# Queries and keys of a hybrid decoder layer projected with features as rows, their head norms taken by a block matrix on TensorE, the stacked layout built by a round trip through DRAM

## The chip, the core and the metric

The kernel runs on one core of a Trainium2 chip. The metric is the time of one execution on the device, in microseconds. A core has TensorE (matrix products; PE in the profile, PEld for its weight loads), VectorE (DVE), ScalarE (ACT), GpSimd (POOL) and SyncE (SP, which issues the DMAs here). TensorE writes PSUM; the others work between PSUM and SBUF. Each engine takes its instructions in a fixed order and waits on semaphores for the others.

## What is computed

One decoder layer over 1024 tokens of width 1024, all in float32. One input projection feeds four mixers, of which differential attention is the one that the change concerns:

```python
h = rms_norm(x, norm1_g)
z = h @ w_in                                  # 1024 x 2304, split into nine parts
q = zq.reshape(b, s, 4, 2, 32)                # 4 heads, 2 maps, 32 features
k = zk.reshape(b, s, 4, 2, 32)
v = zv.reshape(b, s, 4, 64)
...
q = rms_norm(q, q_norm_g)                     # over the 32 features
k = rms_norm(k, k_norm_g)
sc = einsum('bqhmd,bkhmd->bhmqk', q, k) * 32 ** -0.5 + bias      # causal, relative bias
p = softmax(sc)
a = p[:, :, 0] - lam * p[:, :, 1]
o = rms_norm(einsum('bhqk,bkhd->bqhd', a, v), subln_g) * (1 - lam_init)
...
x = x + concatenate([y_pool, y_sconv, y_conf, y_attn]) @ w_out
x = x + (silu(h2 @ w_gate) * (h2 @ w_up)) @ w_down               # h2 = rms_norm(x, norm2_g)
```

## The kernel before

Products keep float32 accuracy by splitting each operand into a rounded part (`hi`) and a remainder (`lo`): `mm3` (L138 to L140) adds hi·hi, hi·lo and lo·hi into one PSUM bank. A weight chunk is loaded by a DMA into `st`, cast to `whi` on ACT (L120), and the remainder `wlo` is made on POOL (L134); there are buffers for three chunks (`wp`, six tiles).

The program goes through these stages: the norm of x and its transposes to `hT`; chunk by chunk (128 features as rows, `wchunk`, `chunk_mm`) the inputs of the conformer, pooling and convolution mixers, with the taps of the depthwise convolution (L317) on DVE as background; then keys, queries and values, each by `proj_tok`, with tokens as rows: for each pair p of token tiles 48 products of 128x256; then attention, 16 units of one pair and one head, into whose gaps products of the output projection (`fillq`, `fill1`, a number from `FQ` at each call) are put; then the second norm and the feed-forward part.

For a pair of keys, `use_k` first calls `ln_pair`, the layer norm of the conformer mixer (transposes into `lnp`, statistics and normalization on DVE, a power on POOL, transposes back, a tanh on ACT), and then `qk_norm`: copy to `qn`, squares, sums over 32 features into a 128x16 tile, the root on POOL (L143, L144), one multiply. Then `stack_T` builds the layout for the scores: for each group g of two heads the four maps are written as 128 columns, the 32 features four times as hi and lo parts (ACT L505, DVE or POOL L506), four 128x128 transposes per token tile on TensorE (L510), and a copy to `KT` (L513). The order of the parts differs between keys (hi, lo, hi, lo) and queries (hi, hi, lo, lo), so that one product over 128 rows gives all four cross terms. Queries go the same way (`use_q`, with the norm weights multiplied in at L530), but only the first pair is stacked before the attention; `prep_q` stacks the others between the units, through PSUM tile `tp` and with calls of `fill1` behind its transposes.

The order on each engine comes from a scheduler of the framework, which ranks by priorities and its own simulated times; DMAs stand in one queue on SP in a fixed order, and each waits there for what it needs.

## Time and profile before

| | us |
|---|---|
| median of 3 runs (lowest, highest) | 1077.91 (1076.92, 1078.37) |
| the profiled execution | 1079.67 |
| its span | 1077.9 |
| TensorE busy | 1047.8 (97%) |
| DVE busy | 736.9 (68%) |
| ACT busy | 439.0 (41%) |
| POOL busy | 223.2 (21%) |

The span is the time from the first to the last instruction of the profiled execution; 1.8 us of it lie around. Busy time of TensorE is that of pipelined products, which overlap: how much one costs is seen from the distance between two starts. A stage is read from its own stretch of the span: which engine has no gap there, and who ends the gaps of the others.

### The profile page before, as it was taken

Reading aid. Unit: us, or ns where it says so; the run is one execution under the profiler, and the core shown is the slowest. Engines: PE = TensorE matmul, PEld = TensorE weight load, DVE = VectorE, ACT = ScalarE, POOL = GpSimd, SP = SyncE. Lnnn points to the kernel's source line nnn. Section 1 sums busy time; section 2 is a strip of 40 time slices with the busy share of each in tenths; the row PEclk is TensorE's granted clock in tenths of the full one; section 3 lists DMA queues with packets and bytes.
Section 4 is the critical chain, followed back from the end, with each engine's and each line's share of the span. In section 5 each row is a group of like instructions: output and inputs, shape, how many; then the busy total and the mean of one; then the engine's idle time right before and its main releaser. Section 6 shows DMA issues by size and latency. Waiting matters only on the chain.

```text
span 1077.9 us, 13508 instructions
## 1 busy us (share of the span) xinstructions
PE 1047.8 (97%) x5203; PEld 876.9 (81%) x5203; DVE 736.9 (68%) x1127; ACT 439.0 (41%) x710; POOL 223.2 (21%) x202
## 2 busy tenths in 40 slices
PE   7999999998989989899999999999999999999998
PEld 6878879996778877788877888888888888888886
DVE  5599995647899966888776776556656567655541
ACT  5512124535786766432332332333333244333320
POOL 5137124655676653000000000000000000000000
PEclk9999999999999999999999999999999999999999
DMA  8131210111021121014576663233223268766731
GB/s 217 49 98 40 59 40 21 40 40 40 30 79 41 50 86 32 6 59 156 220 273 231 218 234 127 59 127 127 88 79 127 102 228 287 261 195 214 230 103 40
DMA packets 89664, 128.04 MB, mean 119 GB/s; under 512 B 17112, under 2 KB 57600, under 8 KB 87040
## 3 DMA queue, kind: packets, MB, share of 16 engines
q1 hardware_dynamic: 89600, 127.18, 35.9%
q8 instruction: 41, 0.67, 0.3%
q14 instruction: 23, 0.19, 0.1%
HBM read 94.13 MB, written 33.04 MB: 118 GB/s over the span
## 4 chain that ended last, share of the span: by engine, by line
PE 74%; DVE 12%; DMA 9%; ACT 2%; issue 1%; POOL 1%; SPq 0%; ACTq 0%; DVEq 0%; POOLq 0%
PE sb L140 8%; PE sb L139 8%; PE sb L138 8%; PE mm L139 6%; PE mm L140 6%; PE mm L138 6%; DMA wd<-in_w_down_dram 4%; PE dx L138 3%; PE dx L140 3%; PE dx L139 3%; DMA dT<-wd 3%; PE dy L138 3%; PE dy L140 3%; PE dy L139 3%; DVE pt L688 1%
## 5 line engine op out<-in xcount | busy, mean ns | idle before, releaser
L138 PE MATMUL sb<-T,rhi 128*128 128x512 f32 x320 | 124.7, 390 | 1.7 <-DVE tp L1030 1.5
L139 PE MATMUL sb<-T,rhi 128*128 128x512 f32 x320 | 124.5, 389 | 0.0
L140 PE MATMUL sb<-T,rlo 128*128 128x512 f32 x320 | 124.3, 389 | 0.0
L911 DVE TENSOR_TENSOR dq<-ds,dq 128x2048 fp32r<-128x2048 f32 x35 | 80.0, 2291 | 61.5 <-ACT dq L910 56.8
L910 ACT CAST dq<-ds 128x2048 fp32r<-128x2048 f32 x35 | 66.9, 1913 | 105.1 <-PE dy L140 38.2
L134 POOL TENSOR_TENSOR wlo<-st,whi 128x1024 fp32r<-128x1024 f32 (+2 forms) x30 | 74.0, 2471 | 109.8 <-ACT whi L120 98.6
L138 PE MATMUL mm<-hT,whi 128*128 128x512 f32 (+1 forms) x224 | 79.6, 367 | 2.3 <-ACT whi L120 1.8
L139 PE MATMUL mm<-hT,whi 128*128 128x512 f32 (+1 forms) x224 | 81.5, 368 | 0.2 <-DVE hT L200 0.2
L140 PE MATMUL mm<-hT,wlo 128*128 128x512 f32 (+1 forms) x224 | 80.7, 364 | 0.4 <-POOL wlo L134 0.4
L138 PEld LDWEIGHTS sb<-T,rhi 128*128 128x128 f32 x320 | 60.1, 188 | 15.0 <-DVE tp L1030 2.5
L317 DVE SCALAR_TENSOR_TENSOR t<-u,cw,t 128x1023 f32<-128x1023 f32 (+28 forms) x58 | 71.4, 1268 | 0.7
L140 PEld LDWEIGHTS sb<-T,rlo 128*128 128x128 f32 x320 | 60.1, 188 | 12.5
L139 PEld LDWEIGHTS sb<-T,rhi 128*128 128x128 f32 x320 | 60.1, 188 | 12.4
L910 ACT CAST rhi<-st 128x1024 fp32r<-128x1024 f32 x28 | 29.5, 1053 | 81.5 <-PE sb L139 49.4
L139 PE MATMUL dx<-dq 128*128 128x512 f32 x160 | 62.2, 389 | 0.0
L140 PE MATMUL dx<-dq 128*128 128x512 f32 x160 | 62.2, 389 | 0.0
L138 PE MATMUL dx<-dq 128*128 128x512 f32 x160 | 61.8, 389 | 0.0
L684 ACT ACTIVATE pt<-sc,mx 128x128 f32<-128x128 f32 (+7 forms) x64 | 47.7, 748 | 18.5 <-DVE mx L681 18.4
L138 PE MATMUL mm<-whi,hT 128*128 128x256 f32 x192 | 54.9, 289 | 0.0
L139 PE MATMUL mm<-wlo,hT 128*128 128x256 f32 x192 | 54.6, 285 | 0.0
L140 PE MATMUL mm<-whi,hT 128*128 128x256 f32 x192 | 54.4, 284 | 0.0
L138 PEld LDWEIGHTS mm<-hT,whi 128*128 128x128 f32 x224 | 42.0, 192 | 10.0 <-ACT whi L120 2.1
(342 smaller groups left out, 2679.6 us busy)
## 6 DMA issues: line engine op xcount, KB each, us to landing
ds<-dL SPq DMA_DIRECT2D x35, 512.0 KB, 4.2
wd<-in_w_down_dram SPq DMA_DIRECT2D x10, 1024.0 KB, 5.0
dT<-wd SPq DMA_DIRECT2D x10, 1024.0 KB, 4.0
dL<-afs SPq DMA_DIRECT2D x10, 1024.0 KB, 4.4
ds<-dT SPq DMA_DIRECT2D x20, 512.0 KB, 6.0
st<-in_w_in_dram SPq DMA_DIRECT2D x18, 512.0 KB, 3.8
st<-in_w_gate_dram SPq DMA_DIRECT2D x15, 512.0 KB, 3.8
st<-in_w_up_dram SPq DMA_DIRECT2D x15, 512.0 KB, 3.7
```

The lines of the kernel that those rows point to most:

```text
L134: G.tensor_tensor(lo[:, nv:], st[:, nv:], hi[:, nv:].bitcast(F), op=ALU.subtract)
L138: T.matmul(ps, lhsT=L[0], rhs=Rr[0], start=first, stop=False, skip_group_check=more)
L139: T.matmul(ps, lhsT=L[0], rhs=Rr[1], start=False, stop=False, skip_group_check=more)
L140: return T.matmul(ps, lhsT=L[1], rhs=Rr[0], start=False, stop=last, skip_group_check=more)
L317: V.scalar_tensor_tensor((z if s == 30 else acc)[:, s:], u[:, :S - s], w[:, 30 - s:31 - s], acc[:, s:], op0=ALU.mult, op1=ALU.add)
L684: A.activation(pts[m][:, 0:w], sc[:, 0:w], AF.Exp, bias=mx, scale=-1.0, accum_out=lt[:, h, m, i:i + 1])
L688: V.scalar_tensor_tensor(pts[0][:, 0:w], pts[1][:, 0:w], cf, pts[0][:, 0:w], op0=ALU.mult, op1=ALU.add)
L910: A.copy(hi, src)
L911: (eng or V).tensor_tensor(lo, src, hi.bitcast(F), op=ALU.subtract)
```

## The change

Keys and queries are projected by `wchunk` and `chunk_mm`, like the other mixers, with 128 features (one group of two heads) as rows and 512 tokens as columns. There are eight such tiles: keys, then queries, each for two groups and two halves of the tokens. The mean square over 32 features is a product with `onr`, a 128x128 matrix of four blocks of 1/32, twice for the hi and lo part of the squares. From it come a root on ACT, a reciprocal on DVE and one further correction step of it (the factor -3 is taken up by the constant 0.25 in `gq`, with the sign). The tile is split into hi and lo, written to DRAM (`kq`), and read back in the stacked order, by four DMAs of 256 KB into `KT` or by eight of 128 KB into `QT`; all eight tiles of `QT` are there before the attention. `qk_norm`, `stack_T`, `prep_q` and the tiles `qn` of the projections go; in the attention the calls of `fill1` that stood in `prep_q` stay. The split tiles use, in turn, the memory of `VV3` and that of `mh` and `ml`; the small `qn` of the attention output takes over a used tile of `QT`. `padl` holds EPS and serves as bias.

```diff
-    gq, gk = bc("gq", q_g, 32, const), bc("gk", k_g, 32, ctp)
-    V.scalar_tensor_tensor(gq, gq, -(32 ** -0.5), gk, op0=ALU.mult, op1=ALU.mult)
+    gq, gk = const.tile([P, 32], F, name="gq")[:, 0:1], ctp.tile([P, 1], F, name="gk")
+    for i in range(4):
+        dma(out=gq[32 * i:32 * (i + 1), :], in_=q_g.rearrange("o p -> p o"))
+        dma(out=gk[32 * i:32 * (i + 1), :], in_=k_g.rearrange("o p -> p o"))
+    V.scalar_tensor_tensor(gq, gq, -0.25 * 32 ** -0.5, gk, op0=ALU.mult, op1=ALU.mult)
...
-    qtp = mid.enter_context(pool("qtp", 2))
+    qtp = mid.enter_context(pool("qtp", 8))
     kvp = mid.enter_context(pool("kvp"))
-    VV = [kvp.tile([P, 2, 4, 128], R, name=f"VV{p}") for p in range(4)]
-    qn = [kvp.tile([P, 2, 256], F, name=f"qn{p}") for p in range(4)]
+    VV = [kvp.tile([P, 2, 4, 128], R, name=f"VV{p}", tag=f"VV{p}") for p in range(3)]
+    QT = {(p, g): qtp.tile([P, 4, 256], R, name="QT", tag="QT") for p in PO for g in range(2)}
...
+    for m in range(4):
+        G.memset(onf[32 * m:32 * (m + 1), 32 * m:32 * (m + 1)], 1.0 / 32)
+    A.copy(onr, onf)
...
+    def heads(c0, isq, order, each=None):
         for g in range(2):
+            W = wchunk(c0 + g * P)
+            for h in order:
+                ps = ps_mm()
+                chunk_mm(W, ps, h, 0, 0, 512)
+                if each:
+                    each(2 * g + h)
+                sh = sm.tile([P, 512], R, name="sh", tag="kn")
+                sl = sm.tile([P, 512], R, name="sl", tag="sq")
+                sq = spp.tile([P, 512], F, name="sqt", tag="sp")
+                A.activation(sh, ps, AF.Square)
+                A.activation(sq, ps, AF.Square)
+                V.tensor_tensor(sl, sq, sh.bitcast(F), op=ALU.subtract)
+                ss = ps_t2()[:, 0:512]
+                T.matmul(ss, lhsT=onr, rhs=sh, start=True, stop=False)
+                T.matmul(ss, lhsT=onr, rhs=sl, start=False, stop=True)
+                r = spp.tile([P, 512], F, name="rt", tag="sp")
+                A.activation(r, ss, AF.Sqrt, bias=padl[:, 0:1])
+                V.reciprocal(r, r)
+                r2 = sq
+                A.activation(r2, r, AF.Square)
+                if isq:
+                    V.scalar_tensor_tensor(r, ps, gq, r, op0=ALU.mult, op1=ALU.mult)
+                else:
+                    V.tensor_tensor(r, ps, r, op=ALU.mult)
+                V.scalar_tensor_tensor(r2, ss, padl[:, 0:1], r2, op0=ALU.add, op1=ALU.mult)
+                V.scalar_tensor_tensor(r, r2, -3.0, r, op0=ALU.add, op1=ALU.mult)
+                n = nh[0]
+                nh[0] += 1
+                hl = (kvp if n % 2 else misc).tile([P, 2, 512], R, name="khl", tag="VV3" if n % 2 else "mh")
+                A.copy(hl[:, 0], r)
+                V.tensor_tensor(hl[:, 1], r, hl[:, 0].bitcast(F), op=ALU.subtract)
+                dma(out=kq[n].rearrange("s p t -> p s t"), in_=hl.bitcast(F))
+                for b in range(2):
+                    for a in range(2):
+                        o = slice(64 * a + 32 * b, 64 * a + 32 * b + 32)
+                        src = kq[n, a if isq else b].rearrange("(m d) t -> d m t", m=4)
+                        if isq:
+                            for k in range(2):
+                                dma(out=QT[2 * h + k, g][o].bitcast(F), in_=src[:, :, 256 * k:256 * (k + 1)])
+                        else:
+                            dma(out=KT[g][o, :, 512 * h:512 * (h + 1)].bitcast(F), in_=src)
...
-    proj_tok(C_K, use_k)
-    proj_tok(C_Q, use_q, PO)
-    for g in range(2):
-        prep_q(PO[0], g, ps_t2, 4)
+    heads(C_K, False, range(2), ln_pair)
+    heads(C_Q, True, range(2))
+    VV.append(kvp.tile([P, 2, 4, 128], R, name="VV3", tag="VV3"))
     proj_tok(C_V, use_v)
...
         if h == PQ1 and j > 0:
-            prep_q(p, 1, ps_tp, 4, fill1)
+            for k in range(2):
+                fill1(marks[-1])
         if h == PQ0 and j < 3:
-            prep_q(PO[j + 1], 0, ps_tp, 4, fill1)
+            for k in range(2):
+                fill1(marks[-1])
         unit(u, p, h)
```

How the instructions stand now is seen at three places. On ACT, before, in the middle of the keys (line numbers of the kernel before; `kst` is the stacked tile, `t` its transpose, `sq` the squares):

```order
L562 ACTIVATE th<-lnp,lb,lg 128x256
L505 CAST kst<-qn_1380 128x8x32 x3
L562 ACTIVATE th<-lnp,lb,lg 128x256
L120 CAST whi<-st 128x1024 x2
L488 COPY qn_1382<-mm 128x512
L505 CAST kst<-qn_1380 128x8x32
L513 CAST KT_1364<-t_1606 128x4x128
L513 CAST KT_1364<-t_1615 128x4x128
L490 ACTIVATE sq<-qn_1382 128x512
```

ACT in the changed kernel (its own line numbers), from the squares of the second key tile to those of the third (`rt` is the root, `khl` the split tile):

```order
L510 ACTIVATE sh<-mm 128x512
L511 ACTIVATE sqt<-mm 128x512
L573 ACTIVATE th<-lnp,lb,lg 128x256
L517 ACT_TABLE_LOAD
L517 ACTIVATE rt<-t_1545,padl 128x512
L520 ACTIVATE sqt<-rt 128x512
L530 CAST khl<-rt 128x512
L573 ACT_TABLE_LOAD
L573 ACTIVATE th<-lnp,lb,lg 128x256
L510 ACTIVATE sh<-mm 128x512
```

Before, work of two pairs was interleaved on ACT; now the squares of a tile stand behind the copy of the tile before, with two table loads in between.

DVE in the changed kernel, from the first reciprocal to the second (`b`, `mv`: statistics of the layer norm):

```order
L518 RECIPROCAL rt<-rt 128x512
L559 BN_AGGR mv<-b_1516 128x2
L559 BN_AGGR mv<-b_1519 128x2
L524 TENSOR_TENSOR rt<-mm,rt 128x512
L525 SCALAR_TENSOR_TENSOR sqt<-t_1467,padl,sqt 128x512
L564 TENSOR_SCALAR ln<-lnp,mv,rs 128x256 x2
L526 SCALAR_TENSOR_TENSOR rt<-sqt,rt 128x512
L531 TENSOR_TENSOR khl<-rt,khl 128x512
L574 TENSOR_SCALAR mixC<-lnp,lg,lb 128x256
L575 SCALAR_TENSOR_TENSOR mixC<-th,mixC 128x256
L512 TENSOR_TENSOR sl<-sqt,sh 128x512
```

The multiply at L524 is the last reader of the projection's bank `mm`; the difference `sl` of the next tile stands behind all that belongs to this one.

TensorE before, around one pair of keys:

```order
L138 MATMUL mm<-whi,hT_101 128x256
L510 MATMUL t_1606<-ident,kst 128x128 x4
L510 MATMUL t_1615<-ident,kst 128x128 x4
L139 MATMUL mm<-wlo,hT_101 128x256
L140 MATMUL mm<-whi,hT_102 128x256
```

TensorE in the changed kernel, at the second key tile's sums (`t_1545`); 22 products of a later tile stand between the last rows shown and the next transposes L568:

```order
L140 MATMUL mm<-hT_103,wlo 128x512
L568 MATMUL lnp<-ident,ln 128x128 x4
L514 MATMUL t_1545<-sh,onr 128x512
L515 MATMUL t_1545<-sl,onr 128x512
L555 MATMUL lnp<-ident,mixC 128x128 x4
L138 MATMUL mm<-hT_101,whi 128x512
```

The transposes of the stacked tiles are gone; the products with the block matrix stand in their place, each behind an operation of ACT or DVE of the same tile.

## Rows read from the trace of the kernel before

**Rows 1.** Page, part 1: busy us, share of the span, instructions

```profile
PE 1047.8 (97%) x5203; PEld 876.9 (81%) x5203; DVE 736.9 (68%) x1127; ACT 439.0 (41%) x710; POOL 223.2 (21%) x202
```

**Rows 2.** Windows: projection stretch, attention; busy us and count by engine, clock, DMA

```profile
163.00:244.00 81.00, 81.00 (x686) 80.76 (x685) 42.73 (x85) 37.17 (x75) 45.94 (x37) 1.00 0.10 33
244.00:410.00 166.00, 154.26 (x852) 126.52 (x851) 144.39 (x366) 115.40 (x266) 102.43 (x100) 0.99 0.17 55
```

**Rows 3.** Timeline of PE in the key projection: start us, duration us, instruction

```profile
180.17 0.28 PE L140 MATMUL mm<-whi,hT 128*128 128x256 f32 x1
180.29 1.03 PE L510 MATMUL t<-ident,kst 128*128 128x128 f32 x8
181.08 0.36 PE L138 MATMUL mm<-whi,hT 128*128 128x256 f32 x1
```

**Rows 4.** Timeline of PE in the chunk projections, 512 columns

```profile
101.22 0.39 PE L138 MATMUL mm<-hT,whi 128*128 128x512 f32 x1
101.45 0.39 PE L139 MATMUL mm<-hT,whi 128*128 128x512 f32 x1
```

**Rows 5.** Groups of PE by form: count, busy us, mean ns, idle before, releaser

```profile
L138 PE MATMUL mm<-whi,hT 128*128 128x256 f32 x192 | 54.9, 289 | 0.0
L510 PE MATMUL t<-ident,kst 128*128 128x128 f32 x80 | 10.8, 272 | 0.0
L510 PE MATMUL tp<-ident,kst 128*128 128x128 f32 x48 | 7.4, 276 | 2.6 <-POOL kst L506 2.6
```

**Rows 6.** Groups of DVE by form

```profile
L536 DVE TENSOR_TENSOR VV<-mm,VV 128x512 fp32r<-128x512 f32 x4 | 2.8, 690 | 9.4 <-ACT VV L535 9.4
L759 DVE SCALAR_TENSOR_TENSOR ml<-tp,subg,mh 128x512 fp32r<-128x512 f32 x4 | 3.0, 746 | 1.1 <-ACT mh L758 1.1
L547 DVE BATCH_NORM_STATS2 b<-lnp 128x6 f32<-128x256 f32 x8 | 3.0, 420 | 1.4 <-PE lnp L544 1.4
L686 DVE RECIPROCAL cf<-lt 128x1 f32<-128x1 f32 x32 | 4.9, 154 | 0.4 <-ACT pt L684 0.3
L349 DVE TENSOR_TENSOR nlam<-es 128x1 f32<-128x1 f32 x1 | 0.1, 148 | 0.0
L350 DVE TENSOR_SCALAR nlam<-nlam 128x1 f32<-128x1 f32 x1 | 0.1, 144 | 0.0
```

**Rows 7.** Groups of ACT by form, then its timeline at the table load

```profile
L490 ACT ACTIVATE sq<-qn 128x512 f32<-128x512 f32 x8 | 5.1, 635 | 0.1
L562 ACT ACTIVATE th<-lnp,lb,lg 128x256 f32<-128x256 f32 x8 | 4.5, 569 | 6.1 <-PE lnp L557 6.0
...
423.62 1.05 ACT L120 CAST whi<-st 128x1024 fp32r<-128x1024 f32 x1 [1.19 <-DMA st<-in_w_up_dram]
424.69 1.28 ACT L917 ACT_TABLE_LOAD   x1
425.99 0.60 ACT L917 ACTIVATE tp<-pg 128x512 f32<-128x512 f32 x1
```

**Rows 8.** Windows behind pauses of TensorE; the column before the last two is the clock

```profile
248.00:252.00 4.00, 2.46 (x11) 1.30 (x10) 3.45 (x12) 1.46 (x7) 2.32 (x3) 1.00 0.19 66
252.00:256.00 4.00, 4.00 (x16) 3.54 (x16) 2.41 (x12) 2.56 (x9) 1.22 (x1) 0.57 0.02 6
```

**Rows 9.** DMA issues (count, KB, us to landing), and SP issuing four

```profile
dL<-afs SPq DMA_DIRECT2D x10, 768.0 KB, 3.3
tr<-scr SPq DMA_DIRECT2D x4, 128.0 KB, 3.3
...
72.66 1.77 SPq L381 DMA_DIRECT2D tr<-scr  x4
```

**Rows 10.** Waits in the attention: us in total, times, longest

```profile
PE tp L510 <- POOL kst L506: 2.6, 3, 1.1
```

**Rows 11.** Chain of waits, 244 to 404 us: first and last piece of the query layout

```profile
264.44 0.70 POOL kst L506
...
354.80 0.44 PE tp L510 x4
```

More of the change, by code (lines that the diff above doesn't have):

```diff
@@ L89, in tile_hybrid @@
     sm = ctx.enter_context(pool("sm"))
-    padl = sm.tile([P, 16], F, name="padl")
+    padl = sm.tile([P, 48], F, name="padl")
     padr = ctx.enter_context(pool("padr", side="right")).tile([P, 56], F, name="padr")
@@ L738, in unit @@
             G.tensor_tensor(rrf, rrf, mhalf[:, 0:8], op=ALU.pow)
+            qn[p] = qtp.tile([P, 2, 256], F, name=f"qn{p}", tag="QT")
             (G if X5[PO.index(p)] else V).tensor_tensor(qn[p].rearrange("p i (h d) -> p (i h) d", h=4), of, rrf.unsqueeze(2).broadcast_to([P, 8, 64]),
@@ L754, in out_attn @@
         yield tr
-        mh = misc.tile([P, 2, 256], R, name="mh", tag="mh")
-        ml = misc.tile([P, 2, 256], R, name="ml", tag="ml")
+        mhl = misc.tile([P, 2, 2, 256], R, name="mh", tag="mh")
+        mh, ml = mhl[:, 0], mhl[:, 1]
         psv = ps.rearrange("p (a b) -> p a b", a=2)
```

46 lines of the change are left out of this document (7 added, 39 removed).

## The prediction

> **What bounds the kernel now.** I read the busy times first, then busy time by stretch, then the order of the instructions, and last the chain of waits of the one stretch that the change also touches. TensorE is busy in 97% of the span [rows 1]; a change pays where it takes columns from TensorE, or a wait from in front of it. The stretch in which queries, keys and values are projected runs from 163.4 us, the first key product, to 244 us, the first score product. In it TensorE never stops (81.00 of 81.00 us) while DVE works 42.73 and ACT 37.17 us [rows 2]. So this stretch costs what TensorE is given there, 80.6 us, and the other two engines have about 40 us of slack each. The attention behind it (244 to 410) is mixed: TensorE 154.26 and DVE 144.39 of 166 us [rows 2]. The feed-forward part, 668 us, is not touched.
>
> **What leaves TensorE.** A product over 256 columns starts 0.12 us after the one before, one over 512 columns 0.227 us (0.23 between two rows; 24 products take 5.45) [rows 3, 4]. Queries and keys now take 384 narrow products, 46.1 us, and will take 192 wide ones, 43.6: 2.5 us less. The transposes of the stacked layout take 0.79 us for eight, 0.87 with the slower first product behind them, so 0.11 each [rows 3]; 80 of them stand in the projection stretch and 48 in the attention [rows 5]: 8.8 and 5.3 us less. Sixteen products with the block matrix come in, 3.6 us more. The demand on TensorE in the projection stretch thus falls by 7.7 us, to 73. If TensorE stayed the bound, that would be the result there.
>
> **What comes to DVE and ACT.** It does not stay the bound. Before, the norm of a group works on sums of 32 (a 128x16 tile), with the root on POOL. Now every one of the eight 128x512 tiles passes a chain at full width: two squares on ACT, their difference on DVE, two products, a root on ACT, a reciprocal on DVE, a square on ACT, three more DVE operations, a copy on ACT, a difference on DVE. The order shows ACT strictly in turn: the squares of the next tile stand behind the copy of this one, and a table is loaded before the root and again before the tanh of the layer norm, eight loads more than before.
>
> The price on which all rests is the reciprocal over 512 elements; no row shows one. The one-element RECIPROCAL takes 154 ns, other one-element operations 144 to 148 [rows 6]. If those 6 to 10 ns are paid once, 512 elements cost what another operation of that size costs, 0.69 us [rows 6]; if they are paid for each element, 3.1 to 5.1 us come on top: 3.8 to 5.8. The others, of two kinds, differ among themselves by 4 ns, and the reciprocal stands apart from both; a surcharge that belongs to the operation is more likely to come with each element than once, so I take an excess of 7 ns, near their mean, per element: 4.3 us. Both ends stay for the range. The Trainium skill, VectorE: DVE Perf Modes, section "First, the fixed hardware budget", says that this operation divides iteratively with a repeat count of 8; by its clock of 0.96 GHz (Trainium Kernel Development and Optimization, section "NeuronCore Architecture") that makes an estimate of 512 x 8 / 0.96 = 4.3 us, the same.
>
> **The projection stretch after the change**, step by step, counted from 163.4:
> - The first root stands on ACT behind the cast of the third weight chunk from there, which waits until the second tile's products release a weight buffer: 48 x 0.227 = 10.9, cast 1.05, table 1.28 [rows 7], root 0.6 (as the square, 635 ns [rows 7]), reciprocal 4.3: 18.1 us.
> - Then three key tiles, each a loop. The reciprocal frees the PSUM bank through one multiply (bank statistics of the layer norm 0.9 and the multiply 0.7 [rows 6]); only then do the 22 products of a later tile run that stand in TensorE's order ahead of the layer norm's transposes (5.0, and 0.6 for the transposes); then tanh, square, square, tanh on ACT (0.5 each), table 1.28, root 0.6, reciprocal 4.3: 15.5 us. Three make 46.5, and 1.0 for one more cast in the first. TensorE needs 6.8 us for a tile: it pauses some 6 us in each loop.
> - Then three query tiles, bound by DVE: 0.69 + 4.3 + 0.75 (with a pointer and from PSUM [rows 6]) x 2 + 0.69 x 2, less 0.3 of overlap = 7.6 each: 22.8. Then the last tile's difference and its ones product, 1.6.
> - Behind that product stand 144 of the 192 value products: 17.3 and 1.3 of waits for banks: 18.6.
> Sum: 18.1 + 47.5 + 22.8 + 1.6 + 18.6 = 108.6 us in place of 80.6: **28 us more**. Each microsecond of the reciprocal is worth seven in this sum. With 0.69 us the first part is 14.5, the loops 11.9 each (36.7 with the cast), the query tiles are bound by TensorE (24 x 0.227 + 0.45 = 5.9 each, 17.7), and the sum is 89.1: 8.5 more. With 5.8 it is 119: 38 more.
>
> The pauses have a second price. From 248 to 252 TensorE was busy for 2.46 of 4 us, and from 252 to 256 its granted clock was 0.57 of full, near the lower of its two levels of 1.2 and 2.4 GHz [rows 8]: 1.7 us lost. Three loops with a pause of 6 us each may lose this three times: **5 us** (0 to 7).
>
> **The round trip.** A tile is written by one DMA of 512 KB and read by four (keys) or eight (queries). DMAs of 768 and 128 KB land after 3.3 us, and SP needs 1.77 us to issue four [rows 9]. So a key tile takes SP about 9 us and a query tile about 11, within the 15.5 of a loop, while query tiles come every 7.6 and queue up: the last is written some 9 us after it is ready. SP waits here for each write before its reads, and behind it queue loads of w_out and the x rows of the partial output projection (not wanted until 10 us into the attention). The scores of the first two heads need the first query tile, some 30 us old by then; those of the other two need the third, which lands about when the stretch ends and is wanted 10 us later. The last buffer of the values shares its memory with odd tiles and waits for the last write, which ends within 1 or 2 us of the last value product. I take **1 us** for this and the exponential's table load together (0 to 4).
>
> **The attention.** Out go 48 transposes, the POOL differences and the ACT copies around them, and with them waits of TensorE for POOL of 2.6 us [rows 10]. In the chain of waits of this stretch thirteen pieces belong to the query layout, 6.0 us together; the first and the last stand in [rows 11]. DVE loses only two operations of 0.4 and stands next in that chain nearly everywhere, so part comes back as waits for DVE: **4 us less** (0 to 10).
>
> The first load of the norm weights, eight tiny DMAs for two, is at 25 us on a queue that waits later anyway: nothing; uncovered it would be 3 us. Both fill slots of a removed layout step are still called: nothing, within 1 us.
>
> **Rivals.**
> - *The reciprocal runs at the ordinary rate.* Stretch +8.5, clock 2, attention -4, start 1: +7.5 us, 1085. For it: nothing shows the long form. Against: the one-element row.
> - *TensorE runs ahead and stays the bound* (faster). Three PSUM banks let it work three tiles ahead, which hides a chain of up to 16 us; then only its demand counts: -7.7, and -6 in the attention: 1064. It decides if the chain of a tile takes less than the 6.8 us of TensorE's work. Against: the in-order ACT queue ties tiles together, and even at 0.69 us the loop is 11.9.
> - *A table switch costs more than the load.* The row shows 1.28 us, with 0.02 us between the cast before it and the load [rows 7]. If the pipe had to empty unseen, each loop, the first root and the exponential would be longer by as much as the load again: five times 1.3, near +7: 1115. The Trainium skill, ScalarE: Activation LUTs, section "What ACT_TABLE_LOAD costs", counts 1.38 us of drain on top of the load for every switch, and its section "Table sets: the hidden batching unit" advises against alternating sets as this change does; the trace's gap does not bear the drain out.
> - *The round trip ends last.* If reads into 32 partitions land in twice the time, the attention waits for its third and fourth heads' queries: some +12 on the forecast, 1120.
>
> **How the numbers follow.** The profiled execution took 1079.7 us (span 1077.9), 1.8 above the median of the runs, 1077.9. Sum: 28 + 5 + 1 - 4 = +30; 1079.7 + 30 = 1109.7, less the 1.8: **1108 us**. Chances: forecast 0.68 (1092 to 1124, reciprocal from 3 to 5.8), ordinary reciprocal 0.14, TensorE as the bound 0.09, table switch 0.05, round trip 0.04. The range goes from the ordinary reciprocal less a bit of attention, 1084, to 1124. About 0.2% can be told from no change here; of the third case 0.02 and of the second 0.01 lie within it, so faster 0.07, same 0.03, slower 0.90.
>
> **What would show it.** A RECIPROCAL row of about 4.3 us, eight of them; DVE busy over 75 us in the projection stretch, and TensorE idle there for some 25 us with waits for ACT and DVE; ACT_TABLE_LOAD rows of 1.28 us, ten in all; a stretch of about 110 us; the attention a few us shorter. Wrong would make it: a reciprocal below 1 us, a PE row that never waits between 165 and 245, or an attention that gains over 10 us.

## The result, and the profile after

The changed kernel takes 1118.73 us (median of five runs, 1116.0 to 1119.61) against 1077.91 (1076.39 to 1078.86) for the kernel before on the same chip: 1.0378 times as long, with an interval of 1.0361 to 1.0396. The forecast was 1108.0 with a range of 1084 to 1124. The profiled execution took 1117.67 us, its span 1115.9.

Three stretches divide the part that matters: the projections (first key product to first score product), the attention (to the first product of the feed-forward part) and the rest (to the end of the span). The first is counted from 163.4 us in every run; the first key product starts at 162.85 us in the kernel before, at 163.10 in the changed one, and between 161.98 and 164.34 in the runs below. Stretches are those of one profiled execution, which for three of the runs (the layer norm moved, the transposes back, the old order) took some 3 us more than the median of the run. A difference of 1 or 2 us between two stretches therefore says nothing.

| stretch, us | before | after | change | forecast |
|---|---|---|---|---|
| projections | 80.6 | 111.8 | +31.2 | +28, clock +5, start +1 |
| attention | 171.6 | 179.6 | +8.0 | -4 |
| rest | 662.3 | 661.1 | -1.2 | 0 |
| span | 1077.9 | 1115.9 | +38.0 | +30 |

The page's first part answers to [rows 1]. TensorE has 304 instructions less and is busy 5 us longer:

```profile
PE 1052.9 (94%) x4899; PEld 864.5 (77%) x4899; DVE 766.0 (69%) x1135; ACT 437.1 (39%) x679; POOL 188.0 (17%) x179
```

The windows of the two stretches after the change (busy us and count of PE, PEld, DVE, ACT and POOL, then the granted clock) answer to [rows 2]:

```profile
163.40:275.20 111.80, 85.96 (x430) 70.36 (x429) 73.55 (x94) 42.82 (x65) 17.34 (x19) 0.86 0.43 126
275.20:454.80 179.60, 159.77 (x829) 126.63 (x828) 147.91 (x374) 111.95 (x253) 95.62 (x92) 0.98 0.18 56
```

In the projections TensorE now stands idle for 25.8 us, where it never stopped before, and runs at a mean clock of 0.86 of full. DVE's work went from 43 to 74 us. The new operations, by form (busy us, mean ns, idle time before them and its releaser), on DVE and ACT:

```profile
L518 DVE RECIPROCAL rt<-rt 128x512 f32<-128x512 f32 x8 | 26.8, 3345 | 2.3 <-ACT rt L517 2.3
...
L517 ACT ACT_TABLE_LOAD x4 | 5.1, 1283 | 0.1
```

The reciprocal takes 3.35 us, five times an ordinary operation of its size. TensorE's waits from 160 to 285 us (us in total, times, longest) name the chain of the norm in all three of their first lines:

```profile
PE mm L138 <- DVE rt L524: 11.6, 3, 5.3
PE t L515 <- DVE sl L512: 8.6, 5, 5.1
PE t L514 <- ACT sh L510: 4.9, 4, 2.9
```

The first of the three loops of the keys, in the chain of waits (start us, us, what). It begins and ends with the multiply that frees the PSUM bank:

```profile
182.13 0.70 DVE rt L524
...
188.47 1.04 ACT whi L120
189.53 1.28 ACT L573
190.82 0.56 ACT th L573
191.39 0.49 ACT sh L510
191.88 0.49 ACT sqt L511
192.36 0.46 ACT th L573
192.83 1.28 ACT L517
194.13 0.70 ACT rt L517
194.85 3.35 DVE rt L518
198.20 0.61 DVE b L558 x2
198.95 0.66 DVE rt L524
199.66 0.79 PE mm L138
200.45 0.43 PE mm L139
```

From multiply to multiply 16.8 us pass: a cast of weights, a table load, a tanh of the layer norm, the squares of the next tile, a tanh, the second load, root, reciprocal. The other two loops take 16.0 and 17.9 us, and in them only the load before the root is in the chain. TensorE's timeline has three pauses in the first, 8.5 us together (start us, us, instruction, idle time before it and its releaser):

```profile
191.93 0.50 PE L514 MATMUL t<-sh,onr 128*128 128x512 f32 x1 [2.87 <-ACT sh L510]
193.14 0.79 PE L515 MATMUL t<-sl,onr 128*128 128x512 f32 x1 [0.71 <-DVE sl L512]
...
199.66 0.79 PE L138 MATMUL mm<-hT,whi 128*128 128x512 f32 x1 [4.87 <-DVE rt L524]
```

The last two rows of the chain show a second price: products of 512 columns follow one another at 0.43 us instead of 0.23 [rows 4], five of them here. The windows there show why (clock in the column before the last two):

```profile
191.00:195.00 4.00, 2.15 (x6) 1.20 (x6) 2.66 (x6) 3.79 (x6) 0.93 (x1) 0.69 1.05 254
195.00:199.00 4.00, 0.00 (x0) 0.00 (x0) 4.00 (x6) 0.63 (x1) 0.00 (x0) 0.50 0.25 91
199.00:203.00 4.00, 3.34 (x8) 2.67 (x9) 3.32 (x7) 1.18 (x2) 0.88 (x2) 0.53 0.00 0
```

With TensorE half busy and then not at all, its clock is granted at the lower of its two levels, and stays there for some microseconds of the work that follows (0.50 and 0.53 in the last two windows). Busy time times the missing share of the clock, summed over windows of 4 us of the whole stretch, makes 8.4 us. I call that sum the clock loss below. Stretch less idle time less clock loss is what TensorE's work takes at full clock: 111.8 - 25.8 - 8.4 = 77.6.

In the attention TensorE's waits are these (275 to 455 us):

```profile
PE sc L684 <- ACT pt L695: 8.3, 11, 1.9
PE tp L710 <- DVE pt L699: 4.6, 5, 2.5
```

The waits for POOL of [rows 10] are gone, and more has come in their place. Before, the same two waits took 1.5 and 1.8 us (244 to 416 us):

```profile
PE tp L699 <- DVE pt L688: 1.8, 4, 0.8
PE sc L673 <- ACT pt L684: 1.5, 2, 0.8
```

TensorE's idle time in the attention rose from 12.3 to 19.8 us and its clock loss from 1.7 to 2.8; the first of these has to be explained, since the change takes 48 transposes and two DVE operations out of there and puts nothing in.

### The profile page after: what moved, and what is told of

The parts are those of the page before. It is cut to its first block, busy times and chain, and to the rows that moved or that the text cites. A ratio compares the mean times of both kernels' runs of the same rounds, so it can differ in the third digit from the quotient of the medians.

```text
span 1115.9 us, 12964 instructions
## 1 busy us (share of the span) xinstructions
PE 1052.9 (94%) x4899; PEld 864.5 (77%) x4899; DVE 766.0 (69%) x1135; ACT 437.1 (39%) x679; POOL 188.0 (17%) x179
## 4 chain that ended last, share of the span: by engine, by line
PE 73%; DVE 12%; DMA 7%; ACT 4%; issue 3%; POOL 1%; SPq 0%; ACTq 0%; DVEq 0%; POOLq 0%
PE sb L138 9%; PE sb L139 9%; PE sb L140 9%; PE mm L138 5%; PE mm L140 5%; PE mm L139 5%; PE dx L138 3%; PE dx L140 3%; PE dx L139 3%; DMA wd<-in_w_down_dram 3%; PE dy L140 2%; PE dy L138 2%; DMA dT<-wd 2%; PE dy L139 2%; DVE rt L518 2%
## 5 line engine op out<-in xcount | busy, mean ns | idle before, releaser
L138 PE MATMUL mm<-hT,whi 128*128 128x512 f32 (+1 forms) x288 | 108.5, 386 | 13.4 <-DVE rt L524 11.6
L139 PE MATMUL mm<-hT,whi 128*128 128x512 f32 (+1 forms) x288 | 108.7, 380 | 0.4 <-DVE hT L200 0.2
L140 PE MATMUL mm<-hT,wlo 128*128 128x512 f32 (+1 forms) x288 | 108.0, 377 | 0.3 <-POOL wlo L134 0.3
L138 PEld LDWEIGHTS mm<-hT,whi 128*128 128x128 f32 x288 | 55.8, 198 | 25.2 <-DVE rt L524 13.2
L140 PEld LDWEIGHTS sb<-T,rlo 128*128 128x128 f32 x320 | 60.5, 189 | 12.6
L139 PEld LDWEIGHTS mm<-hT,whi 128*128 128x128 f32 x288 | 56.7, 197 | 10.6 <-DVE hT L200 1.4
L140 PEld LDWEIGHTS mm<-hT,wlo 128*128 128x128 f32 x288 | 56.6, 196 | 9.9 <-POOL wlo L134 0.6
L120 ACT CAST whi<-st 128x1024 fp32r<-128x1024 f32 x28 | 29.4, 1049 | 60.0 <-PE mm L139 44.6
```

Of the source, the lines that this page charges most:

```text
L120: A.copy(dst, src)
L138: T.matmul(ps, lhsT=L[0], rhs=Rr[0], start=first, stop=False, skip_group_check=more)
L139: T.matmul(ps, lhsT=L[0], rhs=Rr[1], start=False, stop=False, skip_group_check=more)
L140: return T.matmul(ps, lhsT=L[1], rhs=Rr[0], start=False, stop=last, skip_group_check=more)
```

## Experiments

All times are compared with runs of the kernel before on the same chip (medians 1076.5 to 1078.0). The edits are to the changed kernel unless another is named.

**The reciprocal.** It is left out; everything else stays.

```diff
                 A.activation(r, ss, AF.Sqrt, bias=padl[:, 0:1])
-                V.reciprocal(r, r)
```

> The changed kernel with the reciprocal left out (the root itself goes on; this part of the computation is missing). The projection stretch (first key product to first score product) was 80.6 us before and is 111.8 with the change; the reciprocal takes 3.35 us there. Theory A, the stretch is a chain tied together by DVE and ACT in order: seven reciprocals lie on it, so 7 x 3.35 = 23.4 us go as long as the chain stays the bound, plus 2 to 4 us of granted clock that comes back with shorter pauses: a stretch of 84 to 90 us, total 1091 to 1098. Rival B, the pauses belong to the round trip through DRAM and to the lower clock, and the reciprocal hides beside them: under 8 us less, total over 1110.

Measured: 1107.87 us, ratio 1.0286 (1.0266 to 1.0305); stretches 98.8, 181.7, 662.2. The windows of the projections and of the place shown above:

```profile
163.40:262.20 98.80, 84.87 (x430) 70.20 (x429) 47.38 (x87) 42.78 (x65) 17.97 (x19) 0.88 0.48 143
...
191.00:195.00 4.00, 1.92 (x7) 1.40 (x5) 3.89 (x8) 1.55 (x4) 0.83 (x1) 0.60 0.55 165
195.00:199.00 4.00, 4.00 (x11) 3.08 (x11) 1.60 (x3) 1.84 (x2) 0.88 (x2) 0.54 0.34 131
```

The stretch stays far above the one expected. Without the reciprocal 13.0 us of stretch go, 3.9 for each of its microseconds and not seven. TensorE's idle time falls by 11.9, to 13.9, but the clock loss does not fall at all (8.9): the pauses that remain are enough to bring the clock down. 18 us of the 31 remain without any reciprocal. The run changes the order too: by the two timelines about one in nine of TensorE's instructions of the stretch and one in five of DVE's stand in another place, so the 13.0 us are not the price of the reciprocal alone.

**The table loads.** The root becomes a square, so that no set has to be changed between root and tanh.

```diff
-                A.activation(r, ss, AF.Sqrt, bias=padl[:, 0:1])
+                A.activation(r, ss, AF.Square, bias=padl[:, 0:1])
```

> The changed kernel with the root replaced by a square (the right root is missing from the computation), which needs no other function table: eight table loads go, the reciprocal stays. Theory A: the loads of 1.28 us that lie on the chain go, by the trace six of them (one before the first root, one before the first tanh, three before roots, one before the first exponential): 6 to 9 us less, total 1109 to 1113. Rival, a switch drains the pipe and costs twice its row: 13 us or more, total under 1106. Rival, the loads hide beside DVE: under 2 us.

Measured: 1115.23 us, ratio 1.0351 (1.0329 to 1.0373); stretches 110.4, 178.8, 660.7. Seven loads of 1.28 us stood in the stretch and all of them go. The median falls by 3.5 us, which lies between the expectations, the stretch by 1.4 (0.6 when each is counted from its own first key product, 162.32 and 163.10). The order on TensorE, ACT and DVE is nearly the same. The loads stand in the chain above, yet hardly count: when they go, TensorE's wait for DVE's `sl` rises from 8.6 to 10.2 us. Another link was nearly as late; the chain of the second loop now passes through DVE, where `sl` stands behind the end of the layer norm:

```profile
207.72 0.42 DVE mixC L575
208.15 0.67 DVE sl L512
```

In the same loop eleven products follow one another at 0.43 us, where there were five with the loads: part of what the loads gave back went to the clock.

**The layer norm, moved.** Its four pairs go into the values, one with each pair of value tokens.

```diff
     def use_v(p, ps):
...
+        ln_pair(p)
...
-    heads(C_K, False, range(2), ln_pair)
+    heads(C_K, False, range(2))
```

> The changed kernel with the four layer norms called with the value tiles instead of the key tiles; the result is the same. Theory A: the loop of a key tile (16 to 18 us) is tied by ACT, where the layer norm's tanh stands between the squares and the root, and by its table loads; without it key tiles run like query tiles, at 6.3 to 8.3 us, so three loops give back 25 us, the layer norms find 40 us of DVE time under the value products: a stretch of 82 to 90 us, total 1090 to 1098. Rival B, the round trip and SP's queue set the pace (a key tile every 16 us): no gain, total over 1112.

Measured: 1108.69 us, ratio 1.0283 (1.0262 to 1.0304); stretches 91.0, 192.2, 663.3. The stretch of the projections came out just above the 82 to 90 us expected, with 11.6 idle and a clock loss of 5.8. But the scheduler put the last two layer norms into the attention, and there 12.6 us were lost, with the clock at its lower level from 264 to 284 us (windows of that time):

```profile
264.00:274.00 10.00, 7.75 (x29) 6.20 (x30) 8.88 (x40) 5.69 (x21) 1.23 (x4) 0.50 0.00 1
274.00:284.00 10.00, 8.21 (x28) 6.42 (x27) 9.40 (x36) 5.35 (x18) 4.06 (x7) 0.50 0.01 2
```

So the layer norm beside the keys is behind half of the 34 us of idle time and clock loss: 17 are left without it. That it acts through the order on ACT and TensorE is what the chain above shows for one loop; this run also takes half of the layer norms' work out of the stretch, and doesn't tell the two apart.

**The layer norm, first.** All four pairs ahead of the keys.

```diff
-    heads(C_K, False, range(2), ln_pair)
+    for p in range(4):
+        ln_pair(p)
+    heads(C_K, False, range(2))
```

> The changed kernel with all four layer norms called ahead of the key tiles, and none beside them; the result is the same, two of the table loads and the loop through tanh are gone. With the layer norms among the value tiles the stretch fell to 91.0 us, but half of them spilled into the attention, at the lower clock, and that took the gain back. Here nothing can spill. Theory A: the layer norms, one after the other, hold the first root back by some 12 us, then eight tiles follow at DVE's 6.9 us each (reciprocal 3.35, five operations of 0.7), then the value products: a stretch of 92 to 98 us, the attention as with the change (178 to 182), total 1098 to 1105. Rival: the spilled layer norms were not the reason and the attention grows again by over 8 us: total over 1107.

Measured: 1116.87 us, ratio 1.0378 (1.0345 to 1.041); stretches 110.6, 178.9, 660.5. The eight tiles then took about what was expected, 7.3 us each for 6.9 (58.2 from the first reciprocal at 202.99 to 261.2). But the layer norms in a row wait for one another, and TensorE has nothing else to do:

```profile
183.00:203.00 20.00, 6.22 (x19) 3.42 (x19) 10.34 (x26) 6.60 (x12) 1.76 (x4) 0.60 0.01 1
```

The gain and this gap cancel but for 1.2 us of stretch, and the 92 to 98 us expected were missed. The attention did not grow, as the expectation had it.

**Keeping TensorE busy.** Sixteen products without use behind the sums of the first three key tiles, to tell idle time from clock.

```diff
-                ss = ps_t2()[:, 0:512]
+                t2 = ps_t2()
+                ss = t2[:, 0:512]
...
+                if not isq and 2 * g + h < 3:
+                    for k in range(16):
+                        T.matmul(t2[:, 512:1024], lhsT=onr, rhs=sl, start=True, stop=True)
```

> The changed kernel with 16 products more behind the sums of each of the first three key tiles, into a half of a PSUM tile that nobody reads: 48 x 0.227 = 10.9 us of work added to TensorE, in the pauses of some 5 us behind which its clock was 0.50 to 0.53 of full. Theory A: the pauses' second price is the clock; kept busy, TensorE runs the 22 products behind each pause at full clock: each loop 1.5 to 2 us shorter, total 1112 to 1115 in spite of the added work. Rival: the clock is low there for another reason, or the loop does not hang on it: no change or up to 5 us longer.

Measured: 1132.69 us, ratio 1.0519 (1.0494 to 1.0545); stretches 123.8, 182.5, 659.3. Rows of TensorE's timeline (the added products) and of ACT's (the root) show that it tested something else:

```profile
195.90 5.44 PE L519 MATMUL t<-sl,onr 128*128 128x512 f32 x16
```

```profile
201.38 0.69 ACT L521 ACTIVATE rt<-t,padl 128x512 f32<-128x512 f32 x1 [4.84 <-PE t L519]
```

The root reads the first half of the PSUM tile, and waited 4.84 us for products into its second half. The chain was lengthened, and the wait behind it remained. The run tells nothing of the clock.

**The output products that fill gaps.** Twelve calls of the attention get two products more, taken from three late calls. `FQ` is the table of counts; of the six pairs of raised entries the diff shows one, and the three late ones.

```diff
-FQ = [..., 4, 0, 0, 0, 0, 6, ..., 14, 6, 0, 1, 12, 2, 1, 9, ..., 20]
+FQ = [..., 4, 0, 2, 2, 0, 6, ..., 8, 6, 0, 1, 6, 2, 1, 9, ..., 8]
```

> The changed kernel with 24 products of the output projection moved, in the table of numbers, to the six places in the attention where the query transposes stood (two at each of the twelve calls), taken from three late places; the result is the same. The attention (first score product to first feed-forward product) took 171.6 us before and takes 179.6 with the change, though 5.3 us of transposes left it. Theory C: the transposes had stood in gaps where TensorE would have waited, and the table of fill products was fitted to the old gaps; with products put there the attention falls by 3 to 7 us, total 1111 to 1115. Rival D: the attention is longer because something comes late from the projections (query tiles, weight chunks, the x rows behind them on SP's queue): within 1 us of no change, or longer.

Measured: 1130.25 us, ratio 1.0487 (1.0468 to 1.0506); stretches 113.1, 175.4, 677.3. The attention got 4.2 us shorter up to the first feed-forward product, and the rest 16 longer: the products taken from the late calls are missing there (TensorE's clock is 0.61 and 0.54 from 460 to 480 us, 1.00 behind the same point of the changed kernel), and the last product with the values ended at 462.6 us instead of 441.2. Places for fill are not interchangeable.

**Transposes back in the attention.** The removed transposes, with their copies and differences, are put back at their six places on other data.

```diff
+    def old_prep(x3):
+        for i in range(2):
+            st = spp.tile([P, 4, 128], R, name="kst", tag="sp")
...
+            ps = ps_tp()
+            for a in range(4):
+                ins = T.transpose(ps[:, a * P:(a + 1) * P], st[:, a, :].bitcast(F), ident)
+            fill1(ins)
+            A.copy(st, ps.rearrange("p (a b) -> p a b", a=4))
...
-            for k in range(2):
-                fill1(marks[-1])
+            old_prep(X3[2 * j + 1])
```

> The changed kernel with idle work put back into the attention where the query layout stood: at the six places the ACT copies, the DVE or POOL differences and 48 transposes of the kernel before, on data that nobody needs (one buffer is shared with other work, which before it was not). Theory C: what was taken out had cost next to nothing, so putting it back costs next to nothing or helps: attention 170 to 180 us (179.6 without), total 1108 to 1118. Rival D: the attention is long for another reason, and the work put back comes on top: 183 us or more, total over 1121.

Measured: 1117.25 us, ratio 1.0375 (1.0357 to 1.0394); stretches 112.6, 180.1, 662.6. 48 transposes more cost 0.5 us of attention, less than can be told. TensorE is busy 4.2 us longer and idle 3.6 us less (16.2): they fill waits. The attention doesn't go back to 171.6 either, so their number is not what lengthened it.

**The kernel before, with its queries laid out early.** The old operations, transposes included, but all before the attention.

```diff
-    qtp = mid.enter_context(pool("qtp", 2))
+    qtp = mid.enter_context(pool("qtp", 8))
...
         qv = qk_norm(ps, new_qn(p).rearrange("p a b -> p (a b)"))
...
+        for g in range(2):
+            prep_q(p, g, ps_t2, 4)
...
-            prep_q(p, 1, ps_tp, 4, fill1)
+            for k in range(2):
+                fill1(marks[-1])
```

> The kernel before with one part of the change alone: all eight stacked query tiles are built ahead of the attention, by its own path (tokens as rows, transposes on TensorE, no DRAM), in the buffers of the changed kernel (eight query tiles, norm tiles in shared memory); the attention is the changed kernel's. Theory C: the attention is longer because the transposes had stood in gaps of TensorE and the table of fill products was fitted to them: 178 to 183 us here too, in place of 171.6; the projections 5 to 8 us more (48 transposes of 0.11 moved there); total 1088 to 1096. Rival D: the changed kernel's attention suffers from what the projections hand over late: here it takes 165 to 172 us, total 1077 to 1085.

Measured: 1100.7 us, ratio 1.023 (1.0209 to 1.025); stretches 91.9, 181.8, 661.4. Neither round trip nor block matrix is in this kernel, and its attention loses as much as the changed one's:

```profile
255.30:437.10 181.80, 161.96 (x829) 128.82 (x828) 148.41 (x374) 110.92 (x253) 96.76 (x93) 0.96 0.16 50
```

What lengthens the attention is something that both share: the layout work is gone from it, and with it the order may have changed. The next run separates the two.

**The old order in the attention.** The changed kernel, in which each engine takes its instructions of the attention in the order of the kernel before (without those that no longer exist).

```diff
+ORD = {
+    "PE": [0, 1, 2, 3, 4, 5, 6, 7, 15, 14, 8, ...],
...
+    for eng, want in ORD.items():
+        q = [i for i in traced[first:] if str(i.engine) == "EngineType." + eng]
+        for u, v in zip(want, want[1:]):
+            tc.add_manual_dep(q[v], q[u].name, mybir.DependencyInfo(mybir.DependencyClass.NoSync, mybir.DependencyReason.DATA), reason="order")
```

> The changed kernel with the attention's instructions put, engine by engine, into the order of the kernel before (less those of the query layout), by edges that fix nothing but the order of issue; nothing else is changed, the result is the same. The attention took 171.6 us before, 179.6 with the change, 181.8 in the kernel before with its query tiles built early, 180.1 with the transposes put back: neither the projections nor the missing work explain the 8 us. Theory F: the scheduler put the attention into another order once the layout steps were gone, and the tables of fill products fit the old one: with the old order 165 to 172 us, total 1103 to 1111. Rival G: the waits come with the missing steps whatever the order: 177 us or more, total over 1115.

Measured: 1103.49 us, ratio 1.0248 (1.0227 to 1.027); stretches 108.1, 170.0, 663.5. The same instructions take 9.6 us less in the attention:

```profile
271.50:441.50 170.00, 155.65 (x830) 125.36 (x828) 146.84 (x374) 112.19 (x253) 95.98 (x92) 0.99 0.21 63
```

By the timelines, some 590 of 800 instructions of TensorE in the attention stand in the changed kernel in the sequence of the kernel before, and nearly all in this run. Its timeline shows it at one place, the same in both (start us, us, instruction, idle time before it). The changed kernel:

```profile
330.19 0.46 PE L684 MATMUL sc<-KT,QT 128*128 128x512 f32 x1
330.48 0.34 PE L719 MATMUL av<-at,VV 128*128 128x256 f32 x2
330.68 0.41 PE L710 MATMUL tp<-ident,pt 128*128 128x128 f32 x2
332.95 0.62 PE L684 MATMUL sc<-KT,QT 128*128 128x512 f32 x2 [1.87 <-ACT pt L695]
```

With the old order:

```profile
325.05 0.60 PE L690 MATMUL sc<-KT,QT 128*128 128x512 f32 x2
325.48 0.34 PE L725 MATMUL av<-at,VV 128*128 128x256 f32 x2
325.67 0.28 PE L716 MATMUL tp<-ident,pt 128*128 128x128 f32 x1
325.70 0.59 PE L690 MATMUL sc<-KT,QT 128*128 128x512 f32 x2
```

In the first, two transposes (`tp`) stand in a row, and the score products behind them wait 1.87 us for ACT's exponential to leave their buffer; in the second, transposes and pairs of score products alternate, and nothing waits at this place. Over the whole attention the wait for ACT falls from 8.3 to 6.4 us and that of `tp` for DVE from 4.6 to 1.1; idle time (14.4) and clock loss (1.6) together make 6.6 of the 9.6 us. The projections became 3.7 us shorter as well, though nothing ahead of the attention was set and the order on TensorE and ACT is the same. 1.0 of it is the beginning (the first key product starts at 162.11), and 1.8 is one operation of DVE (`rt<-sqt,rt`, L526 of the changed kernel, at 248.69), which takes 0.69 us here and took 2.48 there, beside POOL's remainder of a weight chunk (248.22, 2.40 us).

**A narrow norm.** The sums are taken with tokens as rows (a 128x16 tile), the root on POOL in place of ACT and DVE, spread by ACT and turned by four transposes. This and the next two runs keep the old order in the attention.

```diff
-                T.matmul(ss, lhsT=onr, rhs=sh, start=True, stop=False)
-                T.matmul(ss, lhsT=onr, rhs=sl, start=False, stop=True)
+                for b in range(4):
+                    for k, q in enumerate((sh, sl)):
+                        T.matmul(t2[:, 4 * b:4 * b + 4], lhsT=q[:, b * P:(b + 1) * P], rhs=onr[:, 0:P:32], start=k == 0, stop=k == 1)
...
+                G.tensor_tensor(rr, rr, mhalf[:, 0:16], op=ALU.pow)
+                A.copy(sq.rearrange("p (m d) -> p m d", d=32), rr.unsqueeze(2).broadcast_to([P, 16, 32]))
+                for b in range(4):
+                    T.transpose(t2[:, 512 + b * P:512 + (b + 1) * P], sq[:, b * P:(b + 1) * P], ident)
...
-                V.reciprocal(r, r)
```

> A version that keeps features as rows, the wide products and the round trip, and replaces the norm's chain: the sums of 32 are taken with the tokens as rows (eight products of 4 columns for each tile, a 128x16 tile), the root and its inverse on POOL as in the kernel before, the factors spread by an ACT copy and brought back by four transposes; no table load, no wide reciprocal, no correction step; the attention in the old order. Theory A: what held the projections were the wide DVE and ACT operations in a row: a tile then costs DVE 2.2 us in place of 6.9 and ACT 3.1, TensorE stays the bound with some 78 us: a stretch of 79 to 87 us, total 1071 to 1083. Rival B: the round trip or the small steps' latency (POOL, transposes) holds a tile as long as before: over 95 us, total over 1090.

Measured: 1124.1 us, ratio 1.0435 (1.0417 to 1.0454); stretches 120.5, 168.8, 668.9. DVE's work was halved, and the stretch grew by 12.4 over that with the old order:

```profile
163.40:283.90 120.50, 95.93 (x509) 81.56 (x508) 36.09 (x78) 33.64 (x58) 40.13 (x27) 0.86 0.38 113
```

No engine but TensorE is busy for half of it. TensorE waits in its transposes for the sums that ACT spreads:

```profile
PE t L528 <- ACT sqt L526: 18.1, 6, 5.5
```

The chain has more links, and TensorE's row meets them as early as before. The 79 to 87 us expected were missed by far. The rest, behind the attention, is 6.6 us longer than in the kernel before, which is not accounted for.

**The narrow norm, two tiles behind.** The same operations; TensorE, ACT and DVE get a row in the projections written by hand, in which the sums of a tile stand one tile, and its transposes two tiles, behind its products. The four layer norms, which stood with the four key tiles, are spread over all eight tiles, one with every second.

```diff
+    for n in range(12):
+        m = rec["mm", n]
+        half = len(m) // 2
+        line += m[:half]
+        if n < 8 and n % 2 == 0:
+            line += rec["lnT", n // 2]
+        if 0 <= n - 2 < 8:
+            line += rec["tr", n - 2]
+        if 0 <= n - 1 < 8:
+            line += rec["sum", n - 1]
...
```

> The version with the narrow norm again, its steps put into an order by hand (issue order alone, on TensorE, ACT and DVE): the squares of a tile go ahead of the second half of the tile before, its sums stand in the middle of the next tile's products and its transposes in the middle of the one after that. With the same operations in the scheduler's order the stretch took 120.5 us, with DVE busy under a third and TensorE waiting 16.9 us in front of transposes whose factors were not there yet. Theory A2: in this stretch it is not the amount of work on DVE or ACT that counts but how far behind its products each dependent step stands in TensorE's row; with more than 5 us of products ahead of every step TensorE stays the bound: a stretch of 78 to 87 us, the attention 168 to 172, total 1070 to 1082. Rival: DRAM round trip and POOL (2.9 us for each power, 2.4 for each remainder of weights) hold it: over 95 us, total over 1088.

Measured: 1091.13 us, ratio 1.0141 (1.0124 to 1.0158); stretches 89.8, 169.3, 666.4.

```profile
163.40:253.20 89.80, 84.36 (x513) 73.70 (x512) 40.08 (x79) 32.49 (x58) 40.27 (x27) 0.98 0.59 167
```

Place in the row is worth 30.7 us of stretch here: idle time 24.6 to 5.4, clock loss 13.2 to 1.6. How much of it belongs to the sums and transposes and how much to the layer norms was not told apart. It is the fastest of the kernels with the round trip, and was expected 9 to 21 us faster still: TensorE's work at full clock is 82.8 us, more than the 80.6 of the kernel before, since 64 narrow sums and 32 transposes came in. The rest, behind the attention, is 4.1 us longer than before and not accounted for.

**The changed kernel's own norm, one tile behind.** The same kind of row for TensorE alone, with the change's operations untouched and the layer norms again over all eight tiles.

```diff
+        if n < 8 and n % 2 == 0:
+            line += rec["lnT", n // 2]
+        line += rec.get(("sum", n - 1), [])
...
```

> The changed kernel's own operations, the wide reciprocal and the roots included, with TensorE's row in the projection stretch put into an order by hand: the sums of a tile in the middle of the next tile's products, a layer norm over two tiles, the value products last; the attention in the old order. In the narrow-norm version the hand order took the stretch from 120.5 to 89.8 us. Theory A2: of the 31 us that the change added to this stretch the larger part belongs to the place of the dependent steps in TensorE's row, not to the operations: with the order alone changed DVE becomes the bound (8 x 6.9 us for the tiles, 17 for the layer norms, some 20 us at the start and the end): a stretch of 88 to 97 us, total 1084 to 1094. Theory A, the operations in their chain (reciprocal, tables) are the price: a stretch of 104 us or more, total over 1099.

Measured: 1097.13 us, ratio 1.0182 (1.016 to 1.0205); stretches 103.2, 167.8, 661.5. That lies between the two expectations and decides neither. The reciprocals now come in pairs 8.9 us apart (177.44, 186.29; 198.11, 206.96), but each pair waits for a layer norm, because my row put the transposes of the next one too early:

```profile
PE lnp L509 <- DVE mixC L587: 14.3, 3, 5.3
```

Whether the wide norm can be hidden altogether stays open.

## Where the time went

Work at full clock, idle time and clock loss of the projections, side by side (us):

| kernel | stretch | work | idle | clock loss |
|---|---|---|---|---|
| before | 80.6 | 80.6 | 0 | 0 |
| changed | 111.8 | 77.6 | 25.8 | 8.4 |
| without the reciprocal | 98.8 | 76.0 | 13.9 | 8.9 |
| changed, own row of TensorE | 103.2 | 74.5 | 18.5 | 10.2 |
| narrow norm | 120.5 | 82.7 | 24.6 | 13.2 |
| narrow norm, two tiles behind | 89.8 | 82.8 | 5.4 | 1.6 |

The change does take work from TensorE, by this sum 3 us; the runs with the same work for TensorE there give 74.5 to 77.7 us for it, so 3 to 6. It pays 34 for it in pauses and in the clock behind them.

## Why the prediction was right, and where not

**That the projections lose TensorE as their bound: right.** So was the loop that ties the norm's chain to the layer norm. The parts, against the sum: to the end of the first reciprocal 18.0 us (18.1 forecast); three loops 50.8 (47.5); three query tiles 22.2 (22.8); difference and ones product 1.7 (1.6); values 19.1 (18.6). (The terms of a loop make 15.4 us and not 15.5.) The idle time agrees, 25.8 for 25 forecast, but that is luck: the 25 don't follow from the prediction, whose sum of 108.6 and demand of 73 leave 35.6. The demand fell by 3.0 (77.6 in the table above) and not by 7.7.

**The reciprocal, 4.3 us: mis-sized, 3.35.** That an excess comes with each element is shown; it is (3345 - 690) / 511 = 5.2 ns, just below the low end of the 6 to 10 ns of [rows 6], of which I took the middle. The Trainium skill, VectorE: DVE Perf Modes, section "First, the fixed hardware budget", names a repeat count of 8, from which I had made 4.3 us as well; the 3345 ns don't bear that estimate out. With 3.35 the sum of the stretch would have been 108.6 - 7 x 0.95 = 101.9.

**The clock, 5 us: right for the loops, left out behind them.** The three loops (181.4 to 232.2 us) lost 4.9; another 2.0 went in the query tiles and 1.5 behind them, where the prediction had none, and the 8.4 of the stretch lie above its bound of 7. The pauses of the first loop are not one of 6 us but three, of 2.9, 0.7 and 4.9 (the timeline above).

**What the sum left out, 9.9 us.** With the measured reciprocal the loops would take 44.6 us by the sum, and took 50.8. The products behind the multiply and the layer norm's transposes last 7.2 us in the second loop and 8.2 in the third, where the sum has 5.6: that is mostly the low clock, on the path. In the first loop a second table load is in the chain, 1.3, and in the third a second cast, 0.8. The query tiles would take 20.0 and took 22.2, and 1.8 of that is the operation of DVE at 248.69, which took 2.48 us. The first part is 0.9 longer than its terms. The forecast of 113.6 for stretch and clock came near the 111.8 because the 6.7 us too much for the reciprocal stood against all this. That is luck too.

**"Each microsecond of the reciprocal is worth seven": wrong, 3.9.** The step that failed is the loop as a plain sum. The first part gave back its 3.3 us in full; the three loops, from multiply to multiply, fell from 50.8 to 44.9, by 5.9 in place of 10. With the reciprocal gone, the other links of the loop still make TensorE pause, the clock stays down, and the products in the loop take up to twice their time; part of the difference may be the other order. The rival of the ordinary reciprocal put the stretch 8.5 us above that of before and the clock at 2; the run without any reciprocal lies 18.2 above.

**The table loads on the path, 1.28 in each loop: wrong as a price.** One stands in the chain of each loop, as forecast; without any of the seven, 1.4 us of stretch come back in all, since DVE's `sl` is nearly as late and the clock takes a part. The drain that the rival put beside each load (the Trainium skill, ScalarE: Activation LUTs, section "What ACT_TABLE_LOAD costs") is not seen: 0.02 us lie between the cast's end and the load at 189.53.

**The round trip, 1 us: right.** No wait of TensorE for `KT` or `QT` is in the trace; the last read is issued by 278.6 us, 3.4 after the first score product, and wanted later.

**The attention, 4 us less: wrong in sign, 8.0 more.** The step that failed is that instructions taken out leave the others where they stand. The scheduler ranks anew what is left. With the old order forced the attention takes 170.0 us, so that what was removed is worth 1.6 (not more than can be told apart), within the 0 to 10 stated; the new order costs 9.6. The runs with the early layout (181.8) and with the transposes put back (180.1) show that neither the round trip nor the count of instructions is behind it. Why the scheduler's times lead it to this order was not looked into.

Two of the named signs were missed: DVE is busy for 73.55 us and not over 75, and the attention is not shorter. The rivals "TensorE stays the bound" and "round trip last" have nothing in the trace for them.

## What to carry to other kernels

Where a scheduler sets the order, taking work out of a stretch is not a gain of that work: look at the new order on the engine that bounds the stretch before counting on it, and put the old one back to see what the change itself is worth. A dependent step added beside a bound engine costs by where it stands in that engine's row, not by its sum: the same operations took 120.5 or 89.8 us, depending on where they and the layer norms beside them stood in the rows. Look behind every pause of TensorE for the slower clock, also where the pause became shorter, and measure an operation that no row shows before building a chain on it.

## What was not expected of the hardware

- RECIPROCAL over 512 elements takes 3345 ns, 5.2 ns more per element than an ordinary operation; over one element it takes 154 [rows 6].
- The clock loss is not in proportion to the idle time: 25.8 us idle in the stretch went with a loss of 8.4, 13.9 with 8.9 and 18.5 with 10.2, but 5.4 with 1.6.
- An operation of DVE over 512 elements with two inputs took 2.48 us beside a POOL operation over a 128x1024 tile, against 0.69; with the old order another one took 2.86 (261.85) beside the same kind of POOL operation (261.76). No run tests that POOL is the reason.
- POOL's power over 16 elements takes 2.9 us, over two 0.70 (mean of eight and of four in the narrow norm).
- An ACT instruction that reads one half of a PSUM tile waited in this program for products into its other half, 4.84 us. Whether the chip or the program's semaphores ask for that, the run doesn't tell.
